# First stage of a diffusion step: token sums of squares on TensorE tile by tile, rows of the norm ahead of the first modulation product, finer first loads and a first cast in two parts

## The chip, the cores and the metric

The kernel runs on one core of one Trainium2 chip. The metric is the device time of one execution in microseconds (us). Before the change it is 2034.52 us, the median of 3 runs (2034.43 to 2035.05). One execution was recorded by the hardware profiler; all rows quoted below are from that one.

## The reference, cut to what matters

One layer of a hybrid backbone works on 128 context tokens and 256 latent tokens with 2048 features. Only its beginning matters here: an adaLN modulation (six vectors from a product of SiLU(cond) with a large matrix), an RMSNorm of x with the first two of these vectors, and the projections of the result.

```python
def rmsnorm(x, g):
    y = x * lax.rsqrt(jnp.mean(x * x, axis=-1, keepdims=True) + EPS)
    return y * g

def layer(x, cond, ...):
    mod = jax.nn.silu(cond) @ lw['w_ada'] + lw['b_ada']       # 2048 x 12288
    sh1, sc1, ga1, sh2, sc2, ga2 = split(mod, 6)
    h = rmsnorm(x, lw['norm_pre_mix']) * (1.0 + sc1) + sh1
    m, s_f, s_b = mixer(h, s0_f, s0_b, n_chunks, lw)          # starts with h @ w_in
    x = x + ga1 * rmsnorm(m, lw['norm_post_mix'])
    h = rmsnorm(x, lw['norm_pre_ffn']) * (1.0 + sc2) + sh2
    ff = (silu(h @ lw['w_ffn_gate']) * (h @ lw['w_ffn_up'])) @ lw['w_ffn_down']
    return x + ga2 * rmsnorm(ff, lw['norm_post_ffn']), s_f, s_b
```

## The kernel before

Activations lie transposed: features on the 128 partitions, in 16 tiles (`KT`), and the 384 tokens (`T`) side by side, context tokens first (`segs` is 0 to 128 and 128 to 384). Nearly all of the time after the first stage is matrix products on TensorE. Each float32 product is done as three products of a high part and a low part: an ACT cast makes the high part (`hi`), a DVE subtraction the low part (`lo`); `split` does so for weights and `split_act` (L283) for activations.

The order of PE, ACT, DVE and POOL is the program's own (`manual_schedule`, L129): each engine works through its list in the order in which the lines issue it, and waits where an operand is late. All loads are issued by SP in program order. In this stage each issue also waits until the load eight places before it has landed.

The first stage, L314 to L540, does these things in this order:

- SP loads `cond`, then x in four pieces of four feature tiles (L350, tiles `Chi` and `Clo`), three small tensors, and then for each feature tile `kb` a slab of the modulation matrix (`load_slab`, L322: two halves of 8 feature tiles, 1 MB each, out of 5 buffers) and the weights of the first projections (`load_w`: `raw` 512 KB and `xraw` 128 KB).
- The squares (L433 to L437): ACT squares the 16 feature tiles of x as they land, and DVE adds them up into two accumulators `qs[0]` and `qs[1]`, even and odd tiles.
- `warm(px, 11)` (L440): 11 products with no use for their result, on PE.
- The token sums (L442 to L446): for each of the three groups of 128 tokens, PE multiplies both accumulators (as the stationary operand, 128 columns) with 64 columns of ones, into `px`.
- `gemv(0)`, the modulation product of feature tile 0, is 16 matmuls with 32 stationary columns (L378 to L385). Its first half stands behind the token sums on PE (L447), its second half behind the rows (L453).
- `msx`, `r0`, rows (L448 to L452): DVE takes the mean, ACT and DVE make the reciprocal root, and PE spreads it over all partitions (three matmuls with `ident`). ACT copies that to `rstd` (L455).
- The loop over `kb` (L458): the slab product comes out of PSUM (`ev`, L489), is turned by two small matmuls (L496) into scale and shift of this feature tile (`mods`, L500 and L504), DVE applies them to the tile (`hf`, L506, once per segment of tokens), and `split_act` makes the high and low parts `A_hi`, `A_lo` (L511). The v projection (`vprod`, L399, for each token group two matmuls of 512 columns) and two column tiles of q (`xprod`, L417) of feature tile kb run on PE in the next pass of the loop, around the slab product of that pass (L382).

On the PE list the first `vprod` stands directly behind the L496 matmuls of feature tile 0, then three L417 matmuls, then the slab product of feature tile 1. In the trace every float32 matmul is recorded as two instructions, so that the 11 warm-up matmuls are 22 rows, the 6 token sums 12, and one slab product 32.

Of the kernel before, what the change touches and what calls it, by code (L numbers as in the profile page):

```python
# [11 lines left out]
F32 = mybir.dt.float32  # L12
F32R = mybir.dt.float32r
U32 = mybir.dt.uint32
AF = mybir.ActivationFunctionType
# [5 lines left out]
P = 128  # L21
D = 2048
KT = D // P
TC = 128
TL = 256
T = TC + TL
# [70 lines left out]
def tile_step(ctx: ExitStack, tc: tile.TileContext, a, o):  # L97
    nc = tc.nc
    PE, ACT, DVE, POOL, SP = nc.tensor, nc.scalar, nc.vector, nc.gpsimd, nc.sync
# [9 lines left out]
    spad = const.tile([P, KT, 32], F32, name="spad")  # L109
    POOL.memset(spad, 0.0)  # L110
    eps_t = const.tile([P, 1], F32, name="eps_t")
    ones = const.tile([P, P], F32, name="ones")
# [10 lines left out]
    msx = const.tile([P, 3], F32, name="msx")  # L123
# [7 lines left out]
    segs = ((0, TC, 0), (TC, T, 1))  # L131

    def alloc_A():
        return tuple(actp.tile([P, KT, T], F32R, tag=f"A_{n}", name=f"A_{n}") for n in ("hi", "lo"))
# [4 lines left out]
    def halves(t):  # L139
        tl = [actp.tile([P, 8, T], F32, tag=f"{t}_{n}", name=f"{t}{n}") for n in ("hi", "lo")]  # L140
        return lambda k: tl[k // 8][:, k % 8, :], tl
# [141 lines left out]
    def split_act(hi, lo, src):  # L283
        ACT.copy(hi, src)  # L284
        DVE.tensor_sub(lo, src, hi.bitcast(F32))
# [11 lines left out]
    def warm(dst, n):  # L297

        for _ in range(n):
            PE.matmul(dst, ones, spad.rearrange("p a b -> p (a b)")[:, 0:T], start=True, stop=True)  # L300
# [13 lines left out]
    hT = alloc_A()  # L314
    psm = ctx.enter_context(tc.tile_pool(name="psm", bufs=3, space=PSUM))
    pss = ctx.enter_context(tc.tile_pool(name="pss", bufs=5, space=PSUM))
    with ExitStack() as s:
        pa = s.enter_context(tc.tile_pool(name="pa", bufs=1))
        pb = s.enter_context(tc.tile_pool(name="pb", bufs=2))
        slabs = {}  # L320

        def load_slab(kb):  # L322
            slabs[kb] = [pb.tile([P, KT // 2, 256], F32, tag="slab", name="slab", bufs=5) for _ in range(2)]
            for n, sl in enumerate(slabs[kb]):
                SP.dma_start(sl, a["w_ada1"][kb, :, n * (KT // 2) : (n + 1) * (KT // 2), :])

        xraw = {}

        def load_w(kb):
            load()  # L330
            xraw[kb] = pb.tile([P, XU * P], F32, tag="xraw", name="xraw", bufs=2)
            SP.dma_start(xraw[kb], a["w_x"][kb])
# [14 lines left out]
            return take(), (hi, lo)  # L347

        xn, xnt = halves("C")
        for q in range(4):  # L350
            SP.dma_start(
                xnt[q // 2][:, 4 * (q % 2) : 4 * (q % 2) + 4, :], a["xT"][:, 4 * q : 4 * q + 4, :],
            )
        SP.dma_start(cols, a["b_ada"])
        SP.dma_start(norms, a["norms"])
        cst = pa.tile([P, 2], F32, name="cstA")
# [7 lines left out]
        def load_later():  # L364
            SP.dma_start(wlr, a["w_lr"])
            SP.dma_start(coef[:, 0:2], a["consts"][:, C_COEF : C_COEF + 2])
            SP.dma_start(bgate, a["b_gate"])
            SP.dma_start(gnorm, a["gnorm"])
            SP.dma_start(selr, a["consts"][:, C_SELR : C_SELR + 64])
# [4 lines left out]
        pgm = pss.tile([P, 512], F32, tag="side", name="pgm")  # L374
        pgv, pmod = pgm[:, 0:256], pgm[:, 256:264]
        px = pss.tile([P, T], F32, tag="side", name="px")

        def gemv(kb, ks=range(KT)):  # L378
            slab = slabs[kb]
            for k in ks:  # L380
                q = 32 * (k % 4)
                PE.matmul(  # L382
                    pgv[q : q + 32, :], spad[:, k, :], slab[k // (KT // 2)][:, k % (KT // 2), :],
                    start=k < 4, stop=k >= KT - 4,
                )  # L385
# [28 lines left out]
        def xprod(u, kb, w):  # L414
            def mm():
                for j, (x_, w_) in enumerate(passes(w)):
                    PE.matmul(px, w_[:, u * P : (u + 1) * P], hT[x_][:, kb, :], start=j == 0, stop=j == 2)  # L417

            return mm, lambda dst=None: flush(xacc[u], kb == 0, dst)

        def lrprod(kb):
            def mm():
                for q in range(4):
                    PE.matmul(
                        px[32 * q : 32 * q + 32, :], wlr[:, kb + q, :], scr[:, (kb + q) % 8, :], start=True, stop=True,
                    )

            return mm, lambda dst=None: flush(lracc, kb == 0, dst)

        ACT.activation(spad[:, :, 0:2], cond, AF.Silu)  # L430
        ACT.activation(tmp1, eps_t, AF.Sqrt)
        qs = [pa.tile([P, T], F32, name=f"qsA{n}") for n in range(2)]
        for k in range(KT):  # L433
            sq = qs[k] if k < 2 else scr[:, 4 + k % 4, :]
            ACT.activation(sq, xn(k), AF.Square)
            if k >= 2:
                DVE.tensor_add(qs[k % 2], qs[k % 2], sq)  # L437
        DVE.tensor_scalar_add(bsc1[:, 0, :], cols[:, 1, :], 1.0)
        DVE.tensor_scalar_add(bsc1[:, 1, :], cols[:, 4, :], 1.0)
        warm(px, 11)  # L440

        for t in range(3):  # L442
            for n, q in enumerate(qs):
                PE.matmul(
                    px[:, t * P : t * P + 64], q[:, t * P : (t + 1) * P], ones[:, 0:64], start=n == 0, stop=n == 1,
                )  # L446
        gemv(0, range(KT // 2))  # L447
        DVE.tensor_scalar_mul(msx, px[:, 0:T:P], 1.0 / D)  # L448
        r0 = pa.tile([P, 3], F32, name="r0")
        rsqrt(r0, msx, 1.0)  # L450
        for t in range(3):
            PE.matmul(px[:, t * P : (t + 1) * P], r0[:, t : t + 1].to_broadcast([P, P]), ident, start=True, stop=True)  # L452
        gemv(0, range(KT // 2, KT))  # L453
        rstd = pa.tile([P, T], F32, name="rstdA")
        ACT.copy(rstd, px)  # L455

# [1 line left out]
        for kb in range(KT):  # L458
            if kb and kb + 1 < KT:
                load_slab(kb + 1)  # L460
                load_w(kb + 1)
                if kb == 4:
                    load_later()

            wait = kb in (1, 2)
            if kb and not wait:
                gemv(kb)
            todo = []
            if kb > 4 and kb % 4 == 2:
                todo.append(lrprod(kb - 6))  # L470
            if kb:
                todo += [xprod(u, kb - 1, prev[1]) for u in range(XU)]
            todo += [None] * (4 - len(todo))
            flushes = [t[1] if t else lambda: None for t in todo]

            def pe_x(n):
                if todo[n]:
                    todo[n][0]()

            if wait:  # L480
                vprod(kb - 1, prev[0], (0,))
            pe_x(0)
            hf = scr[:, kb % 8, :]
            DVE.tensor_mul(hf, xn(kb), rstd)
            flushes[0]()
            if wait:
                gemv(kb)
            ev = pb.tile([P, 256], F32, tag="ev", name="ev")
            ACT.copy(ev, pgv)  # L489
            lag = []  # L490
            new = split_w(kb, lag)
            if kb:
                vprod(kb - 1, prev[0], (1 if wait else 0,))
            pm = pmod[:, 4 * (kb % 2) : 4 * (kb % 2) + 4]
            for m in range(2):
                PE.matmul(  # L496
                    pm[:, 2 * m : 2 * m + 2], ev[:, m * P : (m + 1) * P], cst[:, 0:2], start=True, stop=True,
                )
            pe_x(1)
            DVE.tensor_scalar(  # L500
                mods[:, 1, kb, :], pm[:, 2:4], bsc1[:, 0, kb : kb + 1], norms[:, 0, kb : kb + 1],
                op0=ALU.add, op1=ALU.mult,
            )
            DVE.tensor_scalar_add(mods[:, 0, kb, :], pm[:, 0:2], cols[:, 0, kb : kb + 1])  # L504
            for lo, hi, c in segs:
                DVE.tensor_scalar(  # L506
                    hf[:, lo:hi], hf[:, lo:hi], mods[:, 1, kb, c : c + 1], mods[:, 0, kb, c : c + 1],
                    op0=ALU.mult, op1=ALU.add,
                )
            flushes[1]()  # L510
            split_act(hT[0][:, kb, :], hT[1][:, kb, :], hf)  # L511
            if kb:
                if not wait:
                    vprod(kb - 1, prev[0], (1,))
                pe_x(2)
                flushes[2]()
            for sub in lag:
                sub()
            if kb:
                vprod(kb - 1, prev[0], (2,))  # L520
                pe_x(3)
                flushes[3]()
            prev = new
# [72 lines left out]
    with ExitStack() as s:  # L596
# [9 lines left out]
        for c in range(2):  # L606
            src = a["a2"][:, 512 * c : 512 * c + 512]
# [221 lines left out]
    with ExitStack() as s:  # L829
# [158 lines left out]
        for b, i in mix_order:  # L988
# [9 lines left out]
            else:  # L998
# [3 lines left out]
                p = psm.tile([P, T], F32, tag="mm", name="pmm")  # L1002
# [16 lines left out]
    with ExitStack() as s:  # L1019
# [7 lines left out]
        qs = [pe.tile([P, T], F32, tag=f"qs{n}", name="qs", bufs=1) for n in range(3)]  # L1027
# [36 lines left out]
        for i in range(KT):  # L1064
            p = psm.tile([P, T], F32, tag="mm", name="pmm")
            for g in range(2):
                n = 2 * i + g - 2 * KT
# [120 lines left out]
        for k in range(KT + 1):  # L1188
# [7 lines left out]
            if k:  # L1196
                if k % 8 == 1:
                    hw = [take() for _ in range(HEAD)]
                for j, m in ((0, 0), (1, 0), (0, 1)):
                    for u in range(HEAD):  # L1200
                        PE.matmul(  # L1201
                            hp[u], hw[u][j][:, ((k - 1) % 8) * P : ((k - 1) % 8 + 1) * P], h2[m][:, k - 1, :],
                            start=k == 1 and j == m == 0, stop=k == KT and m == 1,
# [24 lines left out]
        for u in range(HEAD):  # L1228
            kind, c, j = ffn_order[u]
# [179 lines left out]
```

## Time and profile before

| what | us |
|---|---|
| median of 3 runs (lowest, highest) | 2034.52 (2034.43, 2035.05) |
| the profiled execution's own time | 2032.79 |
| its span, first to last instruction | 2031.0 |
| PE busy in 0 to 24 us | 17.68 |
| PE busy in 40 to 145 us | 105.0 of 105 |
| DMA over the first 24 us | some 410 GB/s, all 16 engines busy |

The span is what the profiler's rows cover; the execution's own time has 1.79 us around it. In the rows of a timeline the columns are start, duration, engine, line and operation, what is written from what, the count of merged instructions, and in brackets the idle time of that engine just before with what ended it. In the chain of waits each row is a stretch of the path that ended last: start, duration, engine, tile, line. A row of the windows view lists for one stretch of time its length, then the busy time of PE, of PE's weight loads, of DVE, ACT and POOL with the number of instructions, then the granted clock of TensorE as a share of full speed, the busy share of the DMA engines and the rate in GB/s. A busy PE is not PE at its peak: an instruction that mostly loads weights counts as busy too.

### The profile page before, as it was taken

What the parts mean: (1) busy time and instruction counts of PE and PEld (TensorE: products, weight loads), DVE (VectorE), ACT (ScalarE), POOL (GpSimd) and SP (SyncE); (2) the same over time, 40 slices, a digit from 0 to 9 for tenths busy, and PEclk for the clock granted to TensorE, in tenths of its full rate; (3) what the DMA queues carried; (4) which work ended last, traced back from release to release, by engine and by line L of the source; (5) the groups of instructions that cost most, each with busy time, mean ns of one, the idle gap of its engine ahead of it and who ended that gap; (6) DMA issues with size and microseconds to landing.
All of it is one profiled execution on the core that took longest, in us unless ns stands there. A gap on an engine that the chain in (4) does not pass through costs nothing.

```text
span 2031.0 us, 30079 instructions
## 1 busy us (share of the span) xinstructions
PE 2014.6 (99%) x12236; PEld 1959.9 (96%) x12236; DVE 1251.2 (62%) x1655; ACT 770.4 (38%) x1144; POOL 34.2 (2%) x46
## 2 busy tenths in 40 slices
PE   8999999999999999989999999999999999999999
PEld 5779999999999999989999999999999999999998
DVE  5669787898677778866444545453545454544345
ACT  4233545443346544446233222222222222222235
POOL 0000000000000000002000000000000000000001
PEclk9999999999999999999999999999999999999999
DMA  9978677767546785533444444443444444433332
GB/s 390 371 254 276 206 239 233 246 223 261 210 154 207 256 282 185 193 125 115 145 148 147 151 146 147 151 148 125 145 145 146 147 149 150 138 133 125 126 130 97
DMA packets 112395, 373.94 MB, mean 184 GB/s; under 512 B 13692, under 2 KB 32316, under 8 KB 108160
## 3 DMA queue, kind: packets, MB, share of 16 engines
q1 hardware_dynamic: 111248, 370.64, 53.2%
q8 instruction: 96, 1.57, 0.3%
q10 hardware_dynamic: 1008, 1.38, 0.2%
q14 instruction: 43, 0.35, 0.0%
HBM read 358.34 MB, written 13.63 MB: 183 GB/s over the span
## 4 chain that ended last, share of the span: by engine, by line
PE 98%; ACT 1%; DVE 1%; issue 0%; DMA 0%; ACTq 0%; DVEq 0%
PE pmm L258 67%; PE pdn L258 18%; PE pv L399 3%; PE pf L258 2%; PE pgm L382 1%; PE pmm L1201 1%; PE px L417 1%; PE px L300 0%; PE po L629 0%; PE pr L564 0%; PE py L1278 0%; PE pgm L496 0%; PE dl L629 0%; PE pp L856 0%; PE px L870 0%; PE bT L671 0%
## 5 line engine op out<-in xcount | busy, mean ns | idle before, releaser
L258 PE MATMUL pmm<-A_hi,whi 128*128 128x384 f32 x2480 | 831.8, 335 | 0.0
L258 PE MATMUL pmm<-A_hi,wlo 128*128 128x384 f32 x2480 | 828.9, 334 | 0.0
L258 PE MATMUL pmm<-A_lo,whi 128*128 128x384 f32 x2480 | 828.8, 334 | 0.0
L225 DVE TENSOR_TENSOR wlo<-raw,whi 128x1024 fp32r<-128x1024 f32 x434 | 529.8, 1223 | 416.8 <-ACT whi L224 415.6
L224 ACT CAST whi<-raw 128x1024 fp32r<-128x1024 f32 x436 | 457.5, 1050 | 582.4 <-PE pmm L258 226.9
L258 PEld LDWEIGHTS pmm<-A_hi,whi 128*128 128x128 f32 x2480 | 465.6, 188 | 2.9 <-issue 1.8
L258 PEld LDWEIGHTS pmm<-A_lo,whi 128*128 128x128 f32 x2480 | 465.7, 188 | 0.2
L258 PEld LDWEIGHTS pmm<-A_hi,wlo 128*128 128x128 f32 x2480 | 465.6, 188 | 0.0
L556 DVE SCALAR_TENSOR_TENSOR adacc<-adaw,spad,adacc 128x1024 f32<-128x1024 f32 x240 | 296.9, 1278 | 1.2 <-DMA adaw<-in_w_ada 1.0
L258 PE MATMUL pdn<-hid_hi,whi 128*128 128x384 f32 x704 | 235.2, 334 | 0.0
L258 PE MATMUL pdn<-hid_hi,wlo 128*128 128x384 f32 x704 | 235.1, 334 | 0.0
L258 PE MATMUL pdn<-hid_lo,whi 128*128 128x384 f32 x704 | 235.1, 334 | 0.0
L258 PEld LDWEIGHTS pdn<-hid_hi,whi 128*128 128x128 f32 x704 | 132.2, 188 | 0.4 <-issue 0.4
L258 PEld LDWEIGHTS pdn<-hid_lo,whi 128*128 128x128 f32 x704 | 132.2, 188 | 0.0
L258 PEld LDWEIGHTS pdn<-hid_hi,wlo 128*128 128x128 f32 x704 | 132.2, 188 | 0.0
L284 ACT CAST hid_hi<-hfE 128x384 fp32r<-128x384 f32 x44 | 22.6, 513 | 164.0 <-DVE hfE L1224 164.0
L1224 DVE TENSOR_TENSOR hfE<-sg,pmm 128x384 f32<-128x384 f32 x44 | 24.4, 555 | 84.6 <-PE pmm L258 84.0
L1216 ACT ACTIVATE sg<-pmm 128x384 f32<-128x384 f32 x44 | 21.6, 492 | 136.3 <-PE pmm L258 136.2
L1241 DVE TENSOR_TENSOR Blo<-Blo,pdn 128x384 f32<-128x384 f32 x72 | 39.5, 553 | 47.9 <-PE pdn L258 47.9
L1241 DVE TENSOR_TENSOR Bhi<-Bhi,pdn 128x384 f32<-128x384 f32 x72 | 39.1, 549 | 34.1 <-PE pdn L258 34.0
L258 PE MATMUL pmm<-o_hi,whi 128*128 128x384 f32 x128 | 42.8, 335 | 0.0
L258 PE MATMUL pmm<-o_lo,whi 128*128 128x384 f32 x128 | 42.8, 334 | 0.0
(309 smaller groups left out, 1520.9 us busy)
## 6 DMA issues: line engine op xcount, KB each, us to landing
adaw<-in_w_ada SPq DMA_DIRECT2D x128, 512.0 KB, 3.9
raw<-in_w_g SPq DMA_DIRECT2D x88, 512.0 KB, 3.2
raw<-in_w_u SPq DMA_DIRECT2D x88, 512.0 KB, 3.3
raw<-in_w_d SPq DMA_DIRECT2D x88, 512.0 KB, 3.2
slab<-in_w_ada SPq DMA_DIRECT2D x32, 1024.0 KB
raw<-in_w_gate SPq DMA_DIRECT2D x64, 512.0 KB, 4.5
raw<-in_w_in SPq DMA_DIRECT2D x44, 512.0 KB, 3.2
raw<-in_w_out SPq DMA_DIRECT2D x32, 512.0 KB, 4.5
```

The costliest lines, as they stand in the source:

```text
L224: ACT.copy(hi, raw)
L225: sub = lambda: eng.tensor_sub(lo, raw, hi.bitcast(F32))
L258: PE.matmul(dst, w[wi][:, k * n + n0 : k * n + n0 + P], x[xi][:, k0 + k, :], start=first and k == 0 and j == 0, stop=last and k == kts - 1 ...
L284: ACT.copy(hi, src)
L382: PE.matmul(pgv[q : q + 32, :], spad[:, k, :], slab[k // (KT // 2)][:, k % (KT // 2), :], start=k < 4, stop=k >= KT - 4,)
L399: PE.matmul(pv[2 * t + g], hT[x_][:, kb, t * P : (t + 1) * P], w_[:, g * 512 : (g + 1) * 512], start=kb == 0 and j == 0, stop=kb == KT - 1 ...
L417: PE.matmul(px, w_[:, u * P : (u + 1) * P], hT[x_][:, kb, :], start=j == 0, stop=j == 2)
L556: DVE.scalar_tensor_tensor(acc[:, c, :], w, spad[:, k, c : c + 1], acc[:, c, :], op0=ALU.mult, op1=ALU.add,)
L1201: PE.matmul(hp[u], hw[u][j][:, ((k - 1) % 8) * P : ((k - 1) % 8 + 1) * P], h2[m][:, k - 1, :], start=k == 1 and j == m == 0, stop=k == KT ...
L1216: ACT.activation(sgs[j], p, AF.Silu)
L1224: DVE.tensor_mul(hf, sgs.pop(j), p)
L1241: DVE.tensor_add(acc(k), acc(k), p)
```

## The change

Four edits, all in the first stage.

1. Loads: x comes in five pieces (4, 4, 4, 2 and 2 feature tiles) in place of four, and the slab of feature tile 0 in three (8, 4 and 4) in place of two.
2. Sums: DVE still adds the squares of feature tiles 0 to 11 in two accumulators, then adds the two into one, and PE sums that one over the features. The squares of feature tiles 12 to 15 go to PE one by one, three matmuls each, into the same place. The square of tile 15 is made on DVE. All 15 matmuls add onto a matmul with a zeroed stationary operand, which clears `sums` (the first 192 columns of `px`). The warm-up is 7 matmuls, into `pgm`.
3. Order on PE: token sums, rows, then the whole `gemv(0)`, where half of `gemv(0)` stood ahead of the rows.
4. The split of feature tile 0 into high and low part is done once per segment of tokens (128 and 256 columns).

```diff
         def load_slab(kb):
             slabs[kb] = [pb.tile([P, KT // 2, 256], F32, tag="slab", name="slab", bufs=5) for _ in range(2)]
-            for n, sl in enumerate(slabs[kb]):
-                SP.dma_start(sl, a["w_ada1"][kb, :, n * (KT // 2) : (n + 1) * (KT // 2), :])
+            n = KT // 2
+
+            for k0, k1 in ((0, n), (n, 3 * n // 2), (3 * n // 2, KT)) if kb == 0 else ((0, n), (n, KT)):
+                SP.dma_start(slabs[kb][k0 // n][:, k0 % n : k0 % n + k1 - k0, :], a["w_ada1"][kb, :, k0:k1, :])
...
-        for q in range(4):
-            SP.dma_start(
-                xnt[q // 2][:, 4 * (q % 2) : 4 * (q % 2) + 4, :], a["xT"][:, 4 * q : 4 * q + 4, :],
-            )
+        for k0, k1 in ((0, 4), (4, 8), (8, 12), (12, 14), (14, 16)):
+            SP.dma_start(xnt[k0 // 8][:, k0 % 8 : k0 % 8 + k1 - k0, :], a["xT"][:, k0:k1, :])
...
+        zero = pa.tile([P, P], F32, name="zero")
+        POOL.memset(zero, 0.0)
         qs = [pa.tile([P, T], F32, name=f"qsA{n}") for n in range(2)]
+        sums = px[:, 0 : 3 * 64].rearrange("p (t c) -> p t c", t=3)
+
+        def add_sums(src, last=False):
+            for t in range(3):
+                PE.matmul(
+                    sums[:, t, :], src[:, t * P : (t + 1) * P], ones[:, 0:64], start=False, stop=last and t == 2,
+                )
+
+        warm(pgm[:, 0:T], 7)
+        PE.matmul(sums, zero, spad.rearrange("p a b -> p (a b)")[:, 0 : 3 * 64], start=True, stop=False)
         for k in range(KT):
             sq = qs[k] if k < 2 else scr[:, 4 + k % 4, :]
-            ACT.activation(sq, xn(k), AF.Square)
-            if k >= 2:
+            if k == KT - 1:
+                DVE.tensor_mul(sq, xn(k), xn(k))
+            else:
+                ACT.activation(sq, xn(k), AF.Square)
+            if 2 <= k < 12:
                 DVE.tensor_add(qs[k % 2], qs[k % 2], sq)
+            if k == 11:
+                DVE.tensor_add(qs[0], qs[0], qs[1])
+                add_sums(qs[0])
+            if k >= 12:
+                add_sums(sq, k == KT - 1)
...
-        warm(px, 11)
-
-        for t in range(3):
-            for n, q in enumerate(qs):
-                PE.matmul(
-                    px[:, t * P : t * P + 64], q[:, t * P : (t + 1) * P], ones[:, 0:64], start=n == 0, stop=n == 1,
-                )
-        gemv(0, range(KT // 2))
-        DVE.tensor_scalar_mul(msx, px[:, 0:T:P], 1.0 / D)
+        DVE.tensor_scalar_mul(msx, sums[:, :, 0], 1.0 / D)
         r0 = pa.tile([P, 3], F32, name="r0")
         rsqrt(r0, msx, 1.0)
         for t in range(3):
             PE.matmul(px[:, t * P : (t + 1) * P], r0[:, t : t + 1].to_broadcast([P, P]), ident, start=True, stop=True)
-        gemv(0, range(KT // 2, KT))
+        gemv(0)
...
-            split_act(hT[0][:, kb, :], hT[1][:, kb, :], hf)
+            if kb:
+                split_act(hT[0][:, kb, :], hT[1][:, kb, :], hf)
+            else:
+                for lo, hi, c in segs:
+                    split_act(hT[0][:, kb, lo:hi], hT[1][:, kb, lo:hi], hf[:, lo:hi])
```

## The prediction

> **What bounds the kernel now.** I read the page first: the busy shares and the chain of waits by engine.
>
> ```profile
> span 2031.0 us, 30079 instructions
> PE 2014.6 (99%) x12236; PEld 1959.9 (96%) x12236; DVE 1251.2 (62%) x1655; ACT 770.4 (38%) x1144; POOL 34.2 (2%) x46
> PE 98%; ACT 1%; DVE 1%; issue 0%; DMA 0%; ACTq 0%; DVEq 0%
> ```
>
> TensorE is busy for 2014.6 of 2031.0 us and holds 98% of the chain that ended last. A gain or a loss therefore counts where PE waits, or where its list gets longer. The windows view says where that is in the first stage.
>
> ```profile
> 16.00:20.00 4.00, 2.97 (x38) 1.70 (x29) 1.56 (x6) 2.08 (x5) 0.00 (x0) 1.00 1.03 414
> 20.00:24.00 4.00, 2.79 (x21) 2.02 (x25) 3.33 (x6) 0.56 (x2) 0.00 (x0) 1.00 1.02 415
> ...
> 32.00:36.00 4.00, 4.00 (x46) 2.92 (x35) 0.69 (x3) 1.62 (x3) 0.00 (x0) 1.00 1.01 418
> ...
> 40.00:50.00 10.00, 10.00 (x75) 7.77 (x74) 5.53 (x13) 3.23 (x6) 0.00 (x0) 1.00 1.01 409
> ```
>
> PE has holes (busy 2.97 and 2.79 of 4 us) up to some 24 us, and from 32 us it is full. So whatever moves the first projection, which starts at 21.21 us, moves the end by the same amount, if nothing later absorbs it. The DMA engines are full too (share 1.0 or more), with about 410 GB/s: loads can't come earlier. The chain of waits, in order of time, shows what leads to 21.21:
>
> ```profile
> 4.08 10.13 PE px L300 x22
> 14.21 1.28 PE px L444 x12
> 15.50 1.00 PE pgm L382 x16
> 16.50 0.86 PE px L452 x6
> 17.36 1.04 PE pgm L382 x16
> ...
> 18.43 0.38 ACT ev L489
> ...
> 18.86 0.62 PE pgm L496 x4
> ...
> 19.50 0.28 DVE mods L500
> ...
> 19.94 0.68 DVE scr L506 x2
> ...
> 20.64 0.52 ACT A_hi L284
> ...
> 21.21 1.66 PE pv L399 x6
> ```
>
> The columns are start, length, engine and tile. Warm-up until 14.21, token sums 1.28, half of gemv(0) 1.00, rows 0.86, the other half 1.04, then a serial part through ACT, PE and DVE to `A_hi`. The timeline has the engines that feed it:
>
> ```profile
> 8.14 5.87 DVE L437 TENSOR_TENSOR qsA<-qsA,scr 128x384 f32<-128x384 f32 x12 [0.16 <-ACT scr L435]
> 9.53 1.76 ACT L435 ACTIVATE scr<-Clo 128x384 f32<-128x384 f32 x4 [0.18 <-DMA Clo<-in_xT]
> 11.49 1.76 ACT L435 ACTIVATE scr<-Clo 128x384 f32<-128x384 f32 x4 [0.20 <-DMA Clo<-in_xT]
> 9.86 3.74 PEld L300 LDWEIGHTS px<-spad,ones 128*128 128x128 f32 x12 [0.19 <-issue]
> 14.20 2.90 SPq L325 DMA_DIRECT2D slab<-in_w_ada  x2
> 15.54 0.16 DVE L448 TENSOR_SCALAR msx<-px 128x3 f32<-128x3 f32 x1 [1.36 <-PE px L444]
> 16.43 0.93 PE L452 MATMUL px<-ident,r 128*128 128x128 f32 x6
> 23.33 1.93 PE L382 MATMUL pgm<-slab,spad 128*32 128x256 f32 x32
> L437 DVE TENSOR_TENSOR qsA<-qsA,scr 128x384 f32<-128x384 f32 x14 | 6.9, 552 | 7.1 <-ACT scr L435 7.1
> SPq L325 <- DMA slab<-in_w_ada: 5.4, 3, 2.2
> ```
>
> The last two rows are of other views: the group of DVE's additions (0.552 us each) and SP's waits (total, times, longest). ACT squares four tiles in 1.76 us and waits 0.18 to 0.20 us for each piece of x; the last piece is there at 11.45. DVE's last sum ends at 14.01, so that warm-up (14.21) and sums of squares end together. The first half of `gemv(0)` starts at 15.50 and the rows only at 16.43 (PE row): that half fills the wait for mean and root, which lasts from 15.54 to 16.43.
>
> **The change part by part.** *When the first token sum can start.* The twelve DVE additions of tiles 4 to 15 took 5.87 us, the last of 0.55, so the step is (5.87 - 0.55) / 11 = 0.48. That of tile 11 is the eighth: it starts at 8.14 + 7 x 0.48 = 11.5 and ends at 12.1. The new addition of the two accumulators needs its result: 0.03 + 0.55, so 12.7. PE is free by then: of the 22 warm-up rows 14 stay, which end 8 x 0.31 before 14.21, at 11.7 (0.31 from the row with 12 loads in 3.74), and the zero matmul (192 columns, half of a warm-up matmul of 0.62) ends at 12.0. So the shorter warm-up costs nothing while `qs` covers it; without that cover it would be late by what it exceeds 12.7. The squares of tiles 12 to 14 come from ACT by 12.7 to 12.9 and that of tile 15 from DVE at about 13.2 (one more pass of 0.55 behind 12.7).
>
> *How long the sums take.* Before, 6 matmuls (12 rows) took 1.28 us on the path, 0.107 a row. Now there are 15 matmuls, 30 rows: 30 x 0.107 = 3.2 us, from 12.7 to 15.9. PE works at them without a break, since a tile takes it 0.64 us and ACT needs 0.44 for a square: the sums don't end with the last square but 2.7 us behind it. Before they ended at 15.50. That is **+0.40**. I have no row for a matmul that adds onto a third and fourth source; nearest is this same one, with 0.107. The bounds are 0.0625 (a `gemv` row, 16 in 1.00) and 0.143 (a rows matmul, 6 in 0.86): sums from 1.9 to 4.3 us, which end at 14.6 to 17.0, so -0.9 to +1.5 against 15.50.
>
> *The order of PE.* `gemv(0)` filled the wait for the root; now nothing does. From the end of the sums to the rows stay 0.93 us (15.50 to 16.43), the rows take 0.86, and behind them stand all 32 rows of `gemv(0)` instead of 16. By the row of a whole slab product (1.93, of which its second half is 16 steps of 0.058) that is **+0.93**. Behind PE waits `ev`, and behind it on ACT the casts of the first weights, which are needed only with `A_hi`.
>
> *The loads.* SP issues two more loads, and since an issue waits for the load eight places before, the slab comes into the queue later. The queue stays filled all the same: x alone is 3 MB of it until 11.45. The second half of the first slab was there by about 16.7, since the second slab issue in the row of 14.20 (which ends at 17.10) waits for it (the row of SP's waits, up to 2.2 us). `gemv(0)` now begins at 15.9 + 0.93 + 0.86 = 17.7. So both finer loads gain nothing and cost nothing; if the queue ran empty for one issue, it would be some 0.4 us, still before 17.7.
>
> *The cast in two parts.* For its price the groups by form are needed.
>
> ```profile
> L506 DVE TENSOR_SCALAR scr<-scr,mods 128x256 f32<-128x256 f32 x2 | 0.8, 406 | 0.0
> L506 DVE TENSOR_SCALAR scr<-scr,mods 128x128 f32<-128x128 f32 x2 | 0.7, 346 | 0.1
> L284 ACT CAST A_hi<-scr 128x384 fp32r<-128x384 f32 x2 | 1.0, 513 | 2.1 <-DVE scr L506 2.1
> L341 ACT CAST whi<-xraw 128x256 fp32r<-128x256 f32 x1 | 0.4, 408 | 0.0
> ```
>
> The first two `vprod` matmuls need only the first 128 tokens, and in the list of the changed kernel as it is built PE waits for ACT once ahead of the first and once ahead of the third. Their `hf` starts with the row of 19.94 and takes 0.35, instead of 0.68 for both. A cast of 128 columns: 384 take 0.513 and 256 take 0.408, so about 0.30. PE could start at 19.94 + 0.35 + 0.03 + 0.30 + 0.05 = 20.67 instead of 21.21: **-0.54**. Its two matmuls (a third of 1.66, 0.55 us) last until 21.22, and the other segment is ready at 20.64 + 0.41 + 0.04 = 21.09, in time. The two more instructions (one on ACT, one on DVE) lie beside `vprod`. If the second part came late, the gain would shrink to nothing; bounds 0 and -0.6.
>
> *Sum.* 0.40 + 0.93 - 0.54 = **+0.8 us**. The profiled execution goes from 2032.79 (span 2031.0) to 2033.6; the median of the runs stands 1.73 above it, so 2034.52 becomes **2035.3**. That moves the slab product of tile 1 from 23.33 to 24.1, and the loads, which no PE row waits for there, only get more time.
>
> **One rule against a row: the clock.** The sums are the kind of work for which the clock is at risk. A warm-up row streams 384 columns in 0.31 us, so 64 columns need 0.05 of the 0.107: for the rest PE loads weights. Two stretches of this trace show what follows from that.
>
> ```profile
> 2014.00:2016.00 2.00, 1.99 (x13) 1.39 (x12) 0.88 (x4) 1.00 (x3) 0.00 (x0) 1.00 0.01 4
> 2016.00:2018.00 2.00, 1.97 (x9) 1.57 (x9) 0.30 (x2) 0.48 (x1) 0.13 (x1) 0.69 0.00 0
> 2018.00:2020.00 2.00, 2.00 (x4) 1.02 (x4) 2.00 (x5) 0.00 (x0) 1.92 (x3) 0.50 0.00 0
> 2020.00:2022.00 2.00, 2.00 (x6) 0.87 (x5) 2.00 (x6) 0.82 (x2) 1.92 (x3) 0.96 0.48 171
> 2014.51 0.83 PE L292 MATMUL pys<-ones,sq 128*128 128x1 f32 x6
> 900.00:905.00 5.00, 3.38 (x24) 3.27 (x24) 2.29 (x10) 0.93 (x3) 0.00 (x0) 0.90 0.01 5
> 905.00:910.00 5.00, 2.10 (x9) 1.54 (x9) 4.23 (x11) 0.98 (x3) 2.16 (x3) 0.50 0.01 3
> 910.00:915.00 5.00, 5.00 (x18) 5.00 (x19) 4.84 (x12) 4.49 (x10) 3.38 (x4) 0.57 0.00 0
> ```
>
> From 2014 PE is busy for 1.99 and 1.97 of 2 us, with matmuls of a single column, and the granted clock still falls to 0.50, for 3.4 us (0.31, 0.50 and 0.04 lost in three stretches of 2 us, at a loss of a half: 1.24 + 2.0 + 0.16). Around 904, after sums like these ones, it stays at half up to 914. The Trainium skill ("TensorE: Matmul & The Clock Gate", section "What's actually happening") says that the clock goes to half after an idle window of about 3.4 us. By that rule the change keeps full speed, because its longest hole is 0.93 us; by the rows it needn't, since weight loading doesn't seem to count as activity. By the rule the sum is 2035.3, by the rows up to 2036.6.
>
> **The rivals.** *Half clock for one stretch.* In the 3.4 us before the rows begin (13.4 to 16.8), the new order streams about half of 2.5 us, 36%. In the stretch that fell it was less (one-column matmuls for most of it); in 16 to 20 us of before, with 2.97 of 4 us busy, the clock stayed at 1.00. So it is close. Price: rows 1.5 instead of 0.86 and about 1 us of `gemv(0)` doubled, less the part after recovery: +1.3 on top, 2036.6.
>
> *Half clock that lasts*, the slower side: if the clock also stays down over the short first burst at 22 us, as it did from 904 to 914 across holes, then rows and `gemv(0)` double (+2.8) and 1.9 us of the first projection run at half (+0.9): +3.7 on top of +0.8, **2039.0**. It decides from two stretches of 3.4 us on; against it speaks that `gemv(0)` is dense work.
>
> *The sums do overlap* (the row's 0.107 was a wait for both accumulators, not weight loading): the end then follows the square of tile 15, 13.2 + 0.65 = 13.8, 1.7 earlier: -1.7 + 0.93 - 0.54 = -1.3. But the slab of tile 1 lies 2.75 MB behind 16.7 in the queue, at 409 GB/s until 23.4, and half of its product (0.93) must follow: 24.4 instead of 25.3. The gain stops at -0.9: 2033.6. Against it: 12 loads and 12 matmuls were evenly spaced.
>
> *No net effect*: a delay may be taken back later, since the stretch at half clock that begins at 904 ends by time, not by work; 4.5 us of dense matmuls ran in it, and a start 0.8 later spares 0.4 of it. With a price per sum row a little under 0.107 that is 2034.5.
>
> *The later stretches of half clock vanish* because the work falls otherwise on them: up to 4.5 / 2 us of the first, some 1 us for its rows and 3.4 / 2 of the second: -5.0 + 0.8, 2030.3. That is the only way I see to more than 4 us of gain.
>
> **How the numbers follow.** A difference under 0.2% (4.1 us, 2030.45 to 2038.59) can't be told from none. Chances: forecast 2035.3 0.52, half clock for one stretch 0.16, half clock that lasts 0.09, overlapping sums 0.09, no net effect 0.10, vanished stretches 0.04. So slower by more than 0.2% is 0.09, faster 0.04, within 0.87. The range leaves out the lasting half clock and the vanished stretches, and takes in the bounds of a sum row as far as the cases reach: 2033.4 to 2037.0.
>
> **What would show it.** In the changed profile: first token sum at 12.7, 30 sum rows of 0.107 that end at 15.9, nothing on PE until 16.8, `gemv(0)` unbroken from 17.7 to 19.7, the first `vprod` at 22.0 with its third row not waiting, the slab product of tile 1 at 24.1, and the clock at 1.00 to 28 us. Wrong would be: sums that keep step with the squares, a wait of `gemv(0)` for its slab, a clock under 1.00 before 28 us, or a difference at the end that isn't there at 40 us.

## The result and the profile after

| | kernel before | changed kernel |
|---|---|---|
| median, us | 2034.53 | 2038.75 |
| lowest to highest, us | 2032.77 to 2035.92 | 2036.64 to 2042.03 |
| runs | 19 | 19 |
| profiled execution, us | 2032.79 | 2036.98 |
| its span, us | 2031.0 | 2035.2 |

The ratio is 1.0022 with a 95% interval of 1.0015 to 1.0029: slower by 4.2 us at the median. The forecast was 2035.3 with a range of 2033.4 to 2037.0; the measured median lies above it. The profiled pair differs by the same 4.2 us, though both were among the quicker runs of their kernel. Note the spread: the changed kernel varies by 5.4 us, the kernel before by 3.2.

The page of the changed kernel, then the chain of waits of its first stage (start, length, engine, tile, line):

```profile
span 2035.2 us, 30104 instructions
PE 2017.6 (99%) x12248; PEld 1963.2 (96%) x12248; DVE 1250.9 (61%) x1654; ACT 770.2 (38%) x1144; POOL 34.4 (2%) x47
PE 98%; DVE 1%; ACT 1%; DMA 0%; issue 0%; SPq 0%; ACTq 0%; DVEq 0%
```

```profile
12.31 0.57 DVE qsA L455
...
12.93 3.58 PE px L440 x30
...
16.53 0.17 DVE msx L461
...
17.37 0.91 PE px L465 x6
18.28 1.91 PE pgm L382 x32
...
20.21 0.38 ACT ev L502
...
22.11 0.31 ACT A_hi L284
...
22.45 2.09 PE pv L399 x6
24.54 0.96 PE px L417 x3
25.50 2.55 PE pgm L382 x32
```

The sums take 3.58 us instead of 1.28 and end at 16.51 instead of 15.50. PE then has nothing until 17.37, and all of `gemv(0)` follows the rows; `ev` starts at 20.21 instead of 18.43, 1.78 later. The cast in two parts takes 0.54 of that back: the first projection starts at 22.45, 1.24 us later than before. But then the same 6 matmuls take 2.09 us instead of 1.66, the three q products behind them 0.96 instead of 0.54, and the slab product of tile 1 2.55 instead of 1.86. Before, the last two were:

```profile
22.86 0.54 PE px L417 x3
23.40 1.86 PE pgm L382 x32
```

The windows view (busy time of the engines, then granted clock, DMA share, GB/s) has the reason:

```profile
12.00:16.00 4.00, 3.11 (x29) 3.08 (x28) 1.47 (x5) 0.76 (x2) 0.00 (x0) 1.00 0.99 390
16.00:20.00 4.00, 3.12 (x43) 2.03 (x42) 0.90 (x3) 0.78 (x2) 0.00 (x0) 1.00 1.05 427
20.00:24.00 4.00, 2.29 (x14) 1.76 (x11) 2.87 (x8) 2.32 (x5) 0.00 (x0) 0.93 0.99 407
24.00:28.00 4.00, 4.00 (x38) 2.08 (x36) 1.45 (x3) 0.00 (x0) 0.00 (x0) 0.64 1.04 417
900.00:905.00 5.00, 2.97 (x21) 2.87 (x19) 1.46 (x4) 1.33 (x3) 0.00 (x0) 0.91 0.42 142
905.00:910.00 5.00, 4.30 (x19) 3.87 (x18) 2.08 (x10) 0.59 (x2) 0.00 (x0) 0.50 0.00 0
910.00:915.00 5.00, 2.80 (x10) 2.54 (x11) 4.56 (x12) 1.53 (x4) 2.96 (x3) 0.50 0.00 0
915.00:920.00 5.00, 5.00 (x23) 5.00 (x22) 4.84 (x11) 4.72 (x11) 3.06 (x3) 0.72 0.00 0
```

The clock is 0.93 and 0.64 in two stretches of 4 us: at a loss of a half that is (0.07 + 0.36) x 4 x 2 = 3.4 us at half speed, where the trace of before has 1.00 from 12 to 32 us. Later, from 900 to 920 us, it is at half for (0.09 + 0.50 + 0.50 + 0.28) x 5 x 2 = 13.7 us, against (0.10 + 0.50 + 0.43) x 5 x 2 = 10.3 before.

Windows of 1 us put the falls of the clock at 23.48, 904.12 and 2020.28 us. These lie 258 and 327 times 3.413 us apart, so the view can be cut into the stretches in which the clock goes up or down:

```profile
13.24:16.65 3.41, 3.25 (x30) 3.11 (x28) 0.39 (x4) 0.00 (x0) 0.00 (x0) 1.00 1.00 386
20.07:23.48 3.41, 1.70 (x12) 1.34 (x9) 2.35 (x8) 2.32 (x5) 0.00 (x0) 1.00 0.99 411
23.48:26.89 3.41, 3.41 (x22) 2.10 (x24) 1.97 (x3) 0.00 (x0) 0.00 (x0) 0.50 1.07 423
```

The sums fill the first of these, and full clock follows it. Half clock follows the second, with the hole between `gemv(0)` and the first projection. For what PE streams there I estimate, from a warm-up row (384 columns in 0.31 us), that 64 columns take 0.052 of the 0.119 us of a sum row, and count `gemv(0)` and the projections as streaming throughout. Then the first stretch streams about 1.4 us, and the second 1.15 (0.12 of `gemv(0)`, 1.03 of the projection). So in this execution the fall came with the late projection and not straight from the sums. In the kernel before, the stretches lie nearly the same (a fall at 904.02), and the projection, from 21.21 on, fills 2.17 us of the one up to 23.38.

To see what each place costs, three marks on the chain, first of the kernel before and then of the changed one: the first product after the first stage, the first after the second norm, and the long FFN product behind it.

```profile
145.88 16.67 PE pmm L258 x96
...
909.81 27.26 PE pmm L1201 x144
937.08 108.16 PE pmm L258 x624
```

```profile
148.68 16.67 PE pmm L258 x96
...
913.82 27.06 PE pmm L1218 x144
940.88 108.16 PE pmm L258 x624
```

The differences are 2.80, 4.01 and 3.80 us. So in this pair the first stage costs 2.80 (1.24 of longer way and 1.56 of half clock, of which the chain shows 0.43 + 0.42 + 0.69) and the second norm, whose code wasn't touched, 1.00. The last 0.4 up to the span's end come behind the last product.

### The profile page after: what moved, and what is told of

It is laid out like the page before. It is cut to its first block, busy times and chain, and to the rows that moved or that the text cites. A ratio compares the mean times of both kernels' runs of the same rounds, so it can differ in the third digit from the quotient of the medians.

```text
span 2035.2 us, 30104 instructions
## 1 busy us (share of the span) xinstructions
PE 2017.6 (99%) x12248; PEld 1963.2 (96%) x12248; DVE 1250.9 (61%) x1654; ACT 770.2 (38%) x1144; POOL 34.4 (2%) x47
## 4 chain that ended last, share of the span: by engine, by line
PE 98%; DVE 1%; ACT 1%; DMA 0%; issue 0%; SPq 0%; ACTq 0%; DVEq 0%
PE pmm L258 66%; PE pdn L258 18%; PE pv L399 3%; PE pf L258 2%; PE pgm L382 2%; PE pmm L1218 1%; PE px L417 1%; PE po L646 0%; PE pr L581 0%; DMA Chi<-in_xT 0%; PE py L1295 0%; PE pgm L509 0%; PE dl L646 0%; PE pp L873 0%; PE px L887 0%; PE bT L688 0%
```

## The experiments

The theory after the result: the token sums load many weights and stream few columns, PE's activity as the clock sees it falls, and the clock goes to half for one or more stretches of 3.4 us, at a place that differs from execution to execution. The rival: the way to the first projection is longer by 1.24 us, and the rest is chance. As a measure beside the time I use the time lost to half clock, span x (1 - mean granted clock), averaged over a kernel's runs. It was 12.98 us for the changed kernel (19 runs; standard error 0.67), and 9.15 for the kernel before (66 runs; 0.19). A stretch of 3.4 us at half clock counts 1.7 in this measure. It is no pure loss, since half clock also lies over holes of PE; and since a run's clock is recorded in steps of 0.001, which is 2 us, only averages over runs say something.

| run | time, median us | kernel before beside it | ratio, 95% interval | lost to half clock, us |
|---|---|---|---|---|
| e1_cast | 2033.92 | 2035.24 | 0.9986 to 1.0004 | 9.4 |
| e2_order | 2038.07 | 2035.24 | 1.0002 to 1.0020 | 11.7 |
| e3_awake | 2037.62 | 2035.24 | 1.0005 to 1.0022 | 10.2 |
| e4_delay | 2037.09 | 2035.24 | 1.0000 to 1.0018 | 9.8 |
| e5_oldsums | 2035.47 | 2034.73 | 0.9995 to 1.0012 | 9.4 |
| e6_wide | 2035.98 | 2034.73 | 0.9998 to 1.0016 | 9.3 |
| e7_cast_fill | 2034.22 | 2034.73 | 0.9992 to 1.0009 | 8.7 |
| e9_wide_fill | 2036.53 | 2034.73 | 1.0001 to 1.0019 | 9.4 |
| e0_after | 2038.26 | 2034.74 | 1.0011 to 1.0029 | 12.0 |
| e11_narrow | 2041.26 | 2034.74 | 1.0019 to 1.0045 | 15.1 |
| e8_wide_oldloads | 2035.20 | 2034.74 | 0.9996 to 1.0014 | 8.9 |
| e10_best | 2032.78 | 2034.74 | 0.9980 to 0.9998 | 3.1 |

Each kernel has 11 runs (e11_narrow 5), the kernel before beside it 27 to 33; the lost time has a standard error of 0.3 to 0.8. e0_after is the changed kernel again, beside the last three:

> The changed kernel again, on the chip of the three kernels beside it. Both theories: about 4 us over the kernel before, lost time near 13 us. If the chip matters more than the kernel, less than 2.5 us.

It came out 3.5 us over the kernel before, with 12.0 us lost: the kernel makes the difference, not the chip.

### Columns of the token sums: e6_wide, e11_narrow, e5_oldsums

```diff
 # e6_wide, against the changed kernel (e11_narrow: ones[:, 0:16] into sums[:, t, 0:16])
-        sums = px[:, 0 : 3 * 64].rearrange("p (t c) -> p t c", t=3)
+        sums = px.rearrange("p (t c) -> p t c", t=3)
...
-                    sums[:, t, :], src[:, t * P : (t + 1) * P], ones[:, 0:64], start=False, stop=last and t == 2,
+                    sums[:, t, :], src[:, t * P : (t + 1) * P], ones, start=False, stop=last and t == 2,
...
-        PE.matmul(sums, zero, spad.rearrange("p a b -> p (a b)")[:, 0 : 3 * 64], start=True, stop=False)
+        PE.matmul(sums, zero, spad.rearrange("p a b -> p (a b)")[:, 0:T], start=True, stop=False)
```

The last line, which e8_wide_oldloads and e9_wide_fill have too but e11_narrow hasn't, clears the wider `sums`: one matmul of 384 columns instead of 192, ahead of the sums.

> The changed kernel with 128 columns of ones instead of 64 in each token sum: the weights loaded are the same, the streamed columns are doubled. Theory A1 (what counts for the clock is streamed columns): a sum row still takes about 0.12 us, lost time falls to 10 or 11 us, and the time is 1.2 to 2.5 us over the kernel before. Theory A2 (the clock looks at something else, such as whether PE has work at all): lost time stays near 13 us and the time 4 us over the kernel before.

> The changed kernel with 16 columns of ones instead of 64 in each token sum: the same weights loaded, a quarter of the columns streamed. Streaming theory (the clock goes by streamed columns): the sums take the same 3.6 us at full clock, lost time stays at 13 us or rises to 15, and the time is 4 to 6 us over the kernel before. List theory: shorter sums if anything, and 1.2 us over the kernel before.

The chain of e6_wide, then that of e11_narrow:

```profile
12.83 3.63 PE px L440 x30
...
18.24 1.91 PE pgm L382 x32
...
22.41 1.67 PE pv L399 x6
...
24.61 1.86 PE pgm L382 x32
```

```profile
12.83 4.95 PE px L440 x30
...
18.64 1.62 PE px L465 x6
20.27 3.62 PE pgm L382 x32
...
26.55 2.93 PE pv L399 x6
```

With twice the columns a sum row takes 3.63 / 30 = 0.121 us, as with 64 (3.58 / 30 = 0.119): weights set the pace, and the added columns cost nothing. The first projection starts at 22.41, as in the changed kernel. Yet lost time falls from 12 to 13 us to 9.3, and the time to 1.25 us over the kernel before. That agrees with the longer way of 1.24 alone, though the interval is wide (-0.4 to 3.3 us). With a quarter of the columns the sums take 4.95 us, rows, `gemv(0)` and the first projection nearly double (1.62, 3.62, 2.93), and the time is 6.5 us over. In its windows the clock is down from the sums to the slab product of tile 1:

```profile
12.00:16.00 4.00, 3.17 (x23) 3.18 (x23) 1.37 (x5) 0.66 (x2) 0.00 (x0) 0.83 1.01 408
16.00:20.00 4.00, 3.12 (x15) 3.01 (x14) 0.34 (x2) 0.30 (x1) 0.00 (x0) 0.50 1.04 418
20.00:24.00 4.00, 3.84 (x34) 1.39 (x32) 0.56 (x1) 0.58 (x2) 0.00 (x0) 0.50 1.00 409
24.00:28.00 4.00, 2.46 (x8) 2.10 (x8) 2.83 (x8) 2.23 (x5) 0.00 (x0) 0.50 1.06 431
28.00:32.00 4.00, 4.00 (x27) 2.50 (x29) 1.55 (x3) 0.00 (x0) 0.00 (x0) 0.53 0.87 314
```

(0.17 + 0.50 + 0.50 + 0.50 + 0.47) x 4 x 2 = 17.1 us, five times 3.4, with PE busy for 3.84 of 4 us in one of the stretches. Lost time by columns is 15.1 (16), 12 to 13 (64) and 9.3 us (128). The list theory has no place for that: it has the same list three times. I had expected that the sums keep to 3.6 us at 16 columns; in this profile, with most of them at half clock, they take 4.95.

The single profiles agree. Between 12 and 32 us the clock is at half for 3.4 us in the changed kernel and in e0_after, for 10.2 in e2_order and for 6.8 in e3_awake, all with sums of 64 columns, and nowhere in e6_wide, e8_wide_oldloads and e9_wide_fill, with 128. Each of them is one execution, and the stretches of 3.4 us begin elsewhere in each.

```diff
 # e5_oldsums, against the changed kernel: no zero tile, no add_sums; as before
+            ACT.activation(sq, xn(k), AF.Square)
+            if k >= 2:
+                DVE.tensor_add(qs[k % 2], qs[k % 2], sq)
...
+        warm(px, 11)
...
+                    px[:, t * P : t * P + 64], q[:, t * P : (t + 1) * P], ones[:, 0:64], start=n == 0, stop=n == 1,
```

> The changed kernel with the sums of before (DVE adds up all tiles, 6 matmuls, 11 for warm-up); order, loads and cast stay changed. The time lost to half clock is the span times (1 - mean clock): 9.2 us on average in the kernel before, 13.0 in the changed one. Theory A (the token sums, weight loads with little streaming, pull the clock down): lost time back at 9 to 10 us and 0.4 to 1 us over the kernel before. Theory B (the emptier list around the rows does it, with gemv(0) whole behind them): lost time stays near 13 us and 2.5 us or more over the kernel before.

Only 0.74 us over the kernel before, with 9.4 us lost: theory A. (The interval of the time reaches 2.4 us, just under theory B's 2.5; the lost time tells them apart more clearly.) The new order with `gemv(0)` whole behind the rows doesn't by itself pull the clock down.

### Order, delay and loads: e2_order, e4_delay, e8_wide_oldloads

```diff
 # e2_order, against the changed kernel
+        gemv(0, range(KT // 2))
         DVE.tensor_scalar_mul(msx, sums[:, :, 0], 1.0 / D)
...
-        gemv(0)
+        gemv(0, range(KT // 2, KT))
 # e4_delay, against the kernel before
-        warm(px, 11)
+        warm(px, 13)
 # e8_wide_oldloads, against e6_wide: x in four pieces, the slab in two, as before
```

> The changed kernel with the first half of gemv(0) back between the token sums and the mean. List theory (the PE list became 1.24 us longer up to the first projection; the rest is chance in later stretches of half clock): 0.9 us under the changed kernel, about 2037.8. Clock theory (the emptier PE between 16 and 23 us lets the granted clock fall to half, which is the larger part of the 4.2 us): the first projection starts near 21.5, streams for about 2 of the 3.4 us in which the profile of the changed kernel had only 1.05, so the stretch of half clock at 23.4 goes too, and the time is 2 to 3 us under the changed kernel, about 2036.

It is 2.8 us over the kernel before, where the changed kernel is 3.5 to 4.2, with 11.7 us lost: the clock doesn't come back. Whether the 0.9 us of the list do, the intervals don't tell. In its one profile the clock is at half from 14.62 to 21.44 and again from 24.86, and the first projection starts at 24.66 and not at 21.5. This is the stretch ahead of the first fall:

```profile
11.21:14.62 3.41, 1.86 (x17) 1.86 (x17) 2.09 (x6) 1.39 (x4) 0.00 (x0) 1.00 0.99 400
```

All of the 1.86 us are sums, which stream an estimated 0.8. So here half clock lay over the sums themselves, earlier than in the profile of the changed kernel, and the guess that the hole at 21 us alone is to blame was wrong.

> The kernel before with 13 warm-up matmuls instead of 11, a delay of 1.25 us of dense work ahead of everything that follows. List theory and clock theory both: first projection near 22.4, clock 1.00 up to 30 us, about 1.2 us over the kernel before, 2035.8. If a mere shift is what puts the later work badly onto stretches of half clock, it is 2.5 to 4 us over it, as the changed kernel is, with a longer stretch after 900 us.

It came to 1.85 us over at the median (interval 0 to 1.8 thousandths, up to 3.7 us), with 9.8 us lost. But in its profile the delay is not what was meant: the 26 warm-up rows take 10.58 us where 22 had taken 10.13, and the first projection starts at 21.67, 0.46 later than before, and not at 22.4. So what a shift of 1.25 us costs stays open; the interval leaves out the 4.2 us of the changed kernel, but not the 3.5 of e0_after. The expectation of a full clock up to 30 us was wrong too, as a row of its windows and one of its chain show:

```profile
18.29:21.70 3.41, 1.17 (x17) 0.60 (x9) 2.04 (x7) 2.18 (x5) 0.00 (x0) 1.00 1.02 423
21.67 2.93 PE pv L399 x6
```

PE was busy for 1.17 of 3.41 us, behind that the clock is at half for 3.4 us, and the first projection takes 2.93, in a kernel with the sums of before. So those sums aren't free of it in the first stage; but of the six profiles with them (before, e1_cast, e4_delay, e5_oldsums, e7_cast_fill, e10_best) this is the only one that has it there.

> The changed kernel with 128 columns of ones and with the loads of before (x in four pieces, first slab in two). Of the +1.24 us at the first projection, 0.2 is put down to pieces of x that land later: the first token sum then starts near 12.6 or 12.7 instead of 12.8 to 12.9, nothing waits for the slab, and the time is 0 to 0.3 us under that with 128 columns alone. If the last piece of x in two loads does help, the last square is later by 0.4 us or more and the time over it.

The first token sum of e8_wide_oldloads:

```profile
12.88 3.63 PE px L440 x30
...
22.45 1.66 PE pv L399 x6
```

It starts at 12.88, not at 12.6, and the first projection at 22.45, as with the finer loads (12.83 and 22.41). So the finer loads neither gain nor cost here, and my reason for the later first sum (pieces of x that land later) is refuted. The time, 0.46 us over the kernel before, isn't told apart from e6_wide's 1.25 by the intervals.

### The cast alone, and keeping PE at work: e1_cast, e3_awake, e7_cast_fill, e9_wide_fill

```diff
 # e1_cast, against the kernel before: edit 4 of the change alone
 # e3_awake, against the changed kernel (e9_wide_fill: the same on e6_wide; e7_cast_fill: the second part on e1_cast)
+        warm(pgm[:, 0:T], 1)
         DVE.tensor_scalar_mul(msx, sums[:, :, 0], 1.0 / D)
...
                     pm[:, 2 * m : 2 * m + 2], ev[:, m * P : (m + 1) * P], cst[:, 0:2], start=True, stop=True,
                 )
+            if kb == 0:
+                for _ in range(2):
+                    PE.matmul(pgv, ones, spad.rearrange("p a b -> p (a b)")[:, 0:256], start=True, stop=True)
```

> The kernel before with the cast of feature tile 0 in two parts, nothing else. Both theories: the first projection (L399) starts 0.54 us earlier, near 20.7 instead of 21.21, the clock stays at 1.00 up to 30 us, and the time is about 0.5 us under the kernel before. If the two-part cast is itself what lets the clock fall, the time is not under it.

The first projection starts at 20.57 (expected 20.7), 0.64 earlier: 0.54 by the cast, and 0.10 because `gemv(0)` began at 15.40 instead of 15.50 in this execution. The median is 1.3 us under the kernel before; the interval of the ratio (0.9986 to 1.0004) holds the 0.5 us and also nothing. The place is shown, the gain in time is not.

> The changed kernel with matmuls of no use in the two holes of PE: one of 384 columns while the root is made, two of 256 columns while scale and shift of tile 0 are made. Clock theory: granted clock 1.00 from 12 to 30 us, first projection still near 22.45, but the slab product of tile 1 takes 1.9 us again; 1.6 us or more under the changed kernel, at most 2037.2, and with less spread than the 5.4 us of its 19 runs. List theory: the same time as the changed kernel, 2038.7, or more.

> The changed kernel with the 128 columns of ones and with matmuls of no use in both holes (384 columns while the root is made, two of 256 while scale and shift are made). Clock theory: lost time 9 to 10 us, and 1.0 to 1.5 us over the kernel before, which is the longer list alone (first projection at 22.45 instead of 21.21). If lost time stays above 11 us, activity as streamed columns isn't what the clock goes by.

> The kernel before with the cast in two parts and two matmuls of no use (256 columns each) in the hole of PE while scale and shift of tile 0 are made. If some executions of the kernel before lose time to half clock around 21 us: lost time 0.5 to 1.5 us below that of the kernel before, and the time 1.0 to 2.0 us below it. If not: the 0.5 us of the cast and no more, or less where the added matmuls themselves are late.

These three fell short. In e3_awake, where full clock was expected from 12 to 30 us, the clock was at half from 15.34 to 22.16. It fell before the first filler ran (17.54), behind a stretch of 3.41 us with 2.35 us of sums, which stream an estimated 1.0:

```profile
11.93:15.34 3.41, 2.35 (x21) 2.35 (x22) 1.60 (x5) 0.90 (x3) 0.00 (x0) 1.00 1.00 398
```

The other reason is of my own making, and all three have it. The chain of e9_wide_fill:

```profile
20.56 0.61 PE pgm L510 x4
21.16 0.98 PE pgm L515 x4
...
22.18 0.28 DVE mods L517
...
23.35 1.66 PE pv L399 x6
```

DVE's `mods` starts only when the two added matmuls (0.98 us, L515) are done, though it needs only the ones ahead of them. They write the same PSUM tile that it reads, which is the likely reason; no run puts them elsewhere. So the filling went onto the path, and the first projection starts at 23.35 instead of 22.41; e7_cast_fill stands at 21.61 instead of 20.57. Lost time falls in e3_awake from 12 or 13 to 10.2 us and stays at 9.4 in e9_wide_fill, where the columns had done it already. That fits the theory, but the fillers show it less cleanly than the columns.

### A version under both: e10_best

```diff
 # against e1_cast
         wide_sum(pst[0][:, 0], qs[0])
+        warm(prow2, 2)
...
         rows2(prow, 0)
+        warm(prow2, 1)
...
+        warm(hp[1], 2)
         zt = [pss.tile([P, T], F32, tag="side", name="z") for _ in range(2)]
```

> The kernel before with the cast in two parts, and matmuls of no use in the holes of PE in the second norm after 898 us (two, one and two of 384 columns, into PSUM tiles that are free there). There the trace of before has three stretches of half clock (10.2 us) in every execution. Streaming theory: they go or shrink to one, lost time falls from 9.2 to 6 us or less, and the time is 2 to 3.5 us under the kernel before. If the added matmuls hold up the chain through DVE and ACT instead, no gain or a loss of up to 1 us.

The fillers write tiles that no other engine reads until later. Its windows at the second norm:

```profile
900.00:905.00 5.00, 3.75 (x25) 3.65 (x25) 1.96 (x9) 0.93 (x3) 0.00 (x0) 0.82 0.01 4
905.00:910.00 5.00, 3.80 (x15) 2.26 (x15) 4.21 (x11) 0.89 (x3) 2.15 (x3) 0.84 0.00 0
910.00:915.00 5.00, 4.84 (x27) 4.44 (x28) 4.85 (x12) 4.45 (x10) 3.40 (x4) 1.00 0.00 0
```

(0.18 + 0.16) x 5 x 2 = 3.4 us at half clock, where before has 10.3. Lost time, averaged over the runs, is 3.1 instead of 9.2 us, and the median 2032.78 against 2034.74: a gain of 2.0 us (ratio 0.9989, interval 0.9980 to 0.9998), at the lower end of the expected 2 to 3.5. How much of it is the cast's isn't told apart. That it is less than the 6 us of lost time fits half clock that lay over waits for DVE and ACT, which no run separates.

## Why the prediction was wrong

- *Start of the sums*, 12.7: it was 12.93, with the accumulators added at 12.31 (predicted 12.1). It was 0.23 late; e8_wide_oldloads shows that the finer loads aren't the cause, which stays open.
- *Length of the sums*, 0.107 a row and 3.2 us: 0.119 and 3.58. The mechanism was right (weights set the pace, PE falls behind the squares), the term too small by 0.4. With the start that makes +1.01 at their end instead of +0.40.
- *The order*, +0.93: from the end of the sums to the end of `gemv(0)` it was 16.51 to 20.19, 3.68 us, against 15.50 to 18.40 before, 2.90: +0.78. The mechanism was right, with a wait for the root of 0.86. By the prediction's own rows (0.93 + 0.86 + 1.93 against 2.90) the term is 0.82; the 0.93 was a slip.
- *The cast*, -0.54: 0.54 (1.78 late at `ev`, 1.24 at the first projection); the second part wasn't late.
- *The loads*, nothing: nothing, by e8_wide_oldloads.
- So the sum for the way to the first projection, +0.8, was mis-sized by 0.4: +1.24. e6_wide, at the median 1.25 over the kernel before, agrees with this as the cost as long as the clock holds.
- *The clock* is the step that failed. I had the right rows beside it, the stretches at 904 and 2016, and the right mechanism, and then put 0.52 on the full clock and 0.16 and 0.09 on the half. The argument weighed one single stretch, "In the 3.4 us before the rows begin", at 36%, and found "So it is close". That stretch did hold in the profile: 13.24 to 16.65 streamed an estimated 1.4 us, some 42%. The one that fell, 20.07 to 23.48, streamed 1.15, some 34%, and I hadn't looked at it. The prediction says that the "longest hole is 0.93 us", but its own chain leaves PE without work for 1.73 us (19.48 to 21.21), of which 1.22 are left in the changed kernel, and a projection that starts 1.24 later leaves that stretch emptier. In e2_order, e3_awake and e11_narrow it was the stretch at the beginning of the sums that fell. Which one falls differs between executions: the changed kernel's own runs reach from 2036.6 to 2042.0. The price is 1.56 us in the profiled pair in the first stage, and about 2.9 at the median (4.2 less 1.25, or 2.3 by e0_after's 3.5), not +1.3. That 1.3 comes near 1.56 is luck: it was worked out for the rows and `gemv(0)`, and what ran at half was the first projection and the slab product of tile 1.
- *The rule.* In e11_narrow the clock was at half over 20 to 24 us while PE was busy for 3.84 of 4, and in the changed kernel it fell behind a stretch whose longest hole was 1.22 us. The Trainium skill ("TensorE: Matmul & The Clock Gate", section "What's actually happening") gives half clock after an idle window of about 3.4 us; read as a window in which PE has nothing to do, the rule doesn't cover these cases. The same section says that the window runs free of the kernel's start and that the transition differs from run to run. The traces agree: the falls lie 258 and 327 times 3.413 us apart in the changed kernel, and 262 and 326 times in e2_order (14.62, 908.90 and 2021.66), from another start. The prediction left this out of its chances.
- *No net effect later*: the half clock at 900 us was put down as something that takes a delay back. In the profiled pair it cost 1.00 more, one stretch of 3.4 us longer. What it does on average, no run shows by itself.

The likeliest time should have been the one with half clock. With 0.8 corrected to 1.24, the forecast of 2036.6 for one stretch becomes 2037.1, near the quicker runs; the median lies between that and the "half clock that lasts", 2039.0.

## What to carry to other kernels

In these runs a matmul that is bound by its weights wasn't only slow, it also put the clock at risk: where sums over partitions must run on TensorE between dense stretches, give them as many columns as the weights take anyway (128 here, at no cost that the rows show), and look at every stretch of 3.4 us for what it streams, the holes behind the sums included, not only for whether PE is busy. The fillers helped where they wrote PSUM tiles that no engine was waiting for. And a difference of a few microseconds between two profiles can be one stretch of half clock more or less: compare the lost clock over many runs before a cause is named.

## What the runs showed of the hardware

The half clock came in whole stretches of 3.4 us: 3.4, 10.3, 13.7 and 17.1 us in the rows above. Lost time followed streamed columns and not busy time: with the same weights loaded, 16, 64 and 128 columns a matmul lost 15.1, 12 to 13 and 9.3 us, where the kernel before loses 9.15. I hadn't expected that one kernel's runs would differ by 5.4 us, mostly by this: its runs at a mean clock of 0.995 took 2036.6 to 2037.3 us, those at 0.992 took 2040.8 to 2041.5.

The mark below which a stretch counts as idle wasn't measured by a run of its own, but the profiles bound it. By the estimate of streaming used above, the clock fell behind stretches of 3.41 us that streamed 0.2 us (e11_narrow), 0.6 (e4_delay), 0.8 (e2_order), 1.0 (e3_awake), 1.15 (the changed kernel) and 1.26 (e0_after, 20.25 to 23.66, the projection from 22.40 on). It held behind the sums of the changed kernel (1.4) and of e0_after (1.33, 13.42 to 16.83), and behind this stretch of e6_wide, placed by its later fall at 905.04:

```profile
10.75:14.16 3.41, 1.67 (x13) 1.33 (x12) 2.62 (x8) 1.92 (x5) 0.00 (x0) 1.00 1.05 409
```

PE was busy there for 1.67 us only, less than in five of the six stretches behind which the clock fell, but with 128 columns it streamed some 1.5. So the mark lies near 1.3 of 3.41 us here, if the estimate holds; busy time doesn't order these stretches.
